# Sums of weight blocks by an adding load, Silu in one activation, and attention masks one unit later

## The chip, the core and the metric

The kernel runs on one core of a Trainium2 chip. The metric is device time of one execution in microseconds (us). Work is spread over engines that each run their own list of instructions in order: TensorE does the matrix products (PE in the profile, with its weight loads shown apart as PEld), VectorE (DVE) does elementwise arithmetic, ScalarE (ACT) does copies, scaling and activation functions, GpSimd (POOL) issues some transfers and makes index patterns, and SyncE (SP) issues most transfers. Semaphores order the engines among each other. An engine that waits for a semaphore does nothing else until it comes.

## The reference

The reference is a two-layer decoder trunk on 256 tokens of width 2048, in float32. Layer 0 mixes tokens by causal pooling over windows of 2, 4, 8 and 16; layer 1 by 16-head attention in three dilated branches. After each mixer stands a residual sum with a layer norm, then a gated feed-forward with a causal convolution of width 3, and a second residual sum and norm:

```python
u = h @ w_up                                   # 2048 -> 2 * 5504
c = conv_b + sum_j shift(u, j) * conv_w[j]     # depthwise, width 3
gate, val = jnp.split(c, 2, axis=-1)
return (jax.nn.silu(gate) * val) @ w_down      # 5504 -> 2048
```

Here silu(x) is x times sigmoid(x). The change touches the loading of `w_down`, the sigmoid of `gate`, and the tables from which attention masks its scores.

## The kernel before

**Units.** All matrix work is cut into units, a list built ahead of time in the order in which they are to run. Most units own one weight block of 512 rows by 512 columns, 1 MB, held as a tile `raw` of 128 partitions by 4 row blocks by 512 columns. To keep float32 accuracy on the TensorE's float32r inputs, each block is split in two: ACT copies `raw` to `wh` (which rounds it) and DVE writes the rest, `raw - wh`, to `wl`. The products then use both parts. In an ordinary unit the copy is line L82 and the subtraction L83; its matmuls are L165 and L166.

**Order.** `run_units` takes one unit after another. At unit i, `ahead(i)` first issues the loads up to unit i+5 (`do_load`, L72, on SP) and then the splits up to unit i+3; then come the unit's matmuls, then whatever was put off with `later(n, ...)` until this unit, then the unit's own follow-up (`post`). Every engine gets its instructions in this written order and runs them in it. There are three `raw` buffers and four pairs `wh`, `wl`, so SP's next load waits until a `raw` has been split, and ACT's next copy waits until TensorE is through with a `wh`.

**Seven products.** For most row blocks of `w_down` the kernel uses a Strassen-like scheme (the Winograd form): a block of activations and a block of weights are each seen as two by two sub-blocks, and seven products of sums of sub-blocks replace eight. The seven products of one weight block are done in two units that share one `raw`: the "a" unit with three of them and the "b" unit with four. The "b" unit has no load of its own. The sums of weight sub-blocks are made in `split_sums`, in place in `raw`. With r11, r12 (first two row blocks, left and right 256 columns) and r21, r22 (last two), the "a" split does: ACT copies r11, r21 and r22 to `wh` (L103, two instructions); DVE subtracts r11 from r12 (L104); DVE makes `wl` (L106, two instructions); DVE subtracts r12 from r22 (L107); DVE subtracts r22 from r11 and r21 at once (L109). The "b" split then copies and subtracts all four (L96 on ACT, L97 on DVE, two each). There are 58 such blocks, 28 in layer 0 and 30 in layer 1.

**Weaving.** The feed-forward's down-projection is done in chunks of row blocks: chunk 0 has blocks 0 to 2, chunk 1 has 3 to 5, chunk 2 has 6 and 7, chunk 3 the rest. Each chunk runs over four column groups, and the units of one column group are woven between four units of the up-projection (`weave`). In chunk 1 the units of one column group run in the order a3 b3 u a4 b4 u a5 b5 u u, where u is an ordinary up-projection unit, and then the next column group begins with a3 again. Below, this run of ten units is called a cycle of chunk 1; there are four in each layer.

**What follows a column group.** After b5, `early_post` combines the seven products' PSUM banks on DVE (L812 to L819) into tiles `w`, `u3` and `u5`, `tm_post` adds other banks to the stream `HT[c]` (L840, L842), and then POOL adds the three tiles onto `HT[c]` by three adding transfers (L271, `accum_op=OP.add`; in the rows of the profile `ht<-w` of 256 KB and twice `ht<-u` of 128 KB). These wait for the DVE instructions just named, and they are written before the loads of the next `ahead`. In the two column groups of layer 1's chunk 3 that have a seven-product block, `early_post` adds on DVE instead (L822 to L826).

**Gate.** After the convolution of a gate block, `three` (L614 to L617) takes the Sigmoid on ACT into a part of tile `u` (L615), and DVE multiplies it by the convolution's result (L616). This is done 22 times. The product with the value half is L672.

**Masks.** Attention adds a table `negm` and multiplies by a table `cnt`. Each is made in three parts, `masks(0)` to `masks(2)`: an IOTA on POOL and ten small DVE instructions (L1147 to L1159). They are put off until the sixth to eighth turn of the attention stage. In the same turn as `masks(0)`, but behind it, stand the last step of the preceding layer norm (`lo(3)`, L286) and the evacuation of the first key group (`norm_evac`, L446 to L449).

Of the kernel before, what the change touches and what calls it, by code (L numbers as in the profile page):

```python
# [12 lines left out]
AF = mybir.ActivationFunctionType  # L13
OP = mybir.AluOpType
# [4 lines left out]
P = 128  # L19
# [13 lines left out]
def trunk(ctx: ExitStack, tc: tile.TileContext, x, pool_w_in, pool_w_grp, pool_scale, pool_w_out,  # L33
          attn_w_q, attn_w_o, shared_w_k, shared_w_v, ffn_w_up, ffn_conv_w, ffn_conv_b, ffn_w_down,
          ln1_g, ln1_b, ln2_g, ln2_b, out):
    nc = tc.nc
    V, A, PE = nc.vector, nc.scalar, nc.tensor
# [14 lines left out]
    units = []  # L52
    state = {"loaded": 0, "split": 0, "done": 0}
    raw, wh, wl = {}, {}, {}
# [4 lines left out]
    def pieces(i, nk):  # L59
        return [slice(k, k + 1) for k in range(nk)] if i < 4 else [slice(0, nk)]  # L60

    def do_load(i, part=None):
        src = units[i][0]
        if src is None:
            return
        nk, n = src.shape[0] // P, src.shape[1]
        if not part:
            raw[i] = rawp.tile([P, nk, n], F32, name=f"raw{i}", tag="raw")
        rows = src.rearrange("(k p) n -> p k n", p=P)
        ks = pieces(i, nk)  # L70
        for s in ks if part is None else ks[1:] if part else ks[:1]:
            nc.sync.dma_start(raw[i][:, s], rows[:, s])  # L72
# [15 lines left out]
    B1, B2, N1, N2 = slice(0, 2), slice(2, 4), slice(0, 256), slice(256, 512)  # L88

    def split_sums(i, kind):  # L90
        h = wh[i] = wp.tile([P, 4, 512], F32R, name=f"wh{i}", tag="wh")
        l = wl[i] = wp.tile([P, 4, 512], F32R, name=f"wl{i}", tag="wl")
        if kind == "b":
            r = raw.pop(i - 1)
            for n in (N2, N1):
                A.copy(h[:, :, n], r[:, :, n])  # L96
                V.tensor_tensor(l[:, :, n], r[:, :, n], h[:, :, n].bitcast(F32), OP.subtract)  # L97
            return
        r = raw[i]
        r11, r12, r22 = r[:, B1, N1], r[:, B1, N2], r[:, B2, N2]  # L100
        parts = [(slice(0, 4), N1), (B2, N2)]
        for k, n in parts:
            A.copy(h[:, k, n], r[:, k, n])  # L103
        V.tensor_tensor(r12, r12, r11, OP.subtract)  # L104
        for k, n in parts:
            V.tensor_tensor(l[:, k, n], r[:, k, n], h[:, k, n].bitcast(F32), OP.subtract)  # L106
        V.tensor_tensor(r22, r22, r12, OP.subtract)  # L107
        both = r[:, :, N1].rearrange("p (b k) n -> p b k n", b=2)
        V.tensor_tensor(both, both, r22.unsqueeze(1).to_broadcast([P, 2, 2, 256]), OP.subtract)  # L109

# [9 lines left out]
    def later(n, fn):  # L120
        if n == 0:
            fn()
        else:
            pending.append([n, fn])

    def run_units(upto):
        while state["done"] < upto:
            i = state["done"]
            ahead(i)
            for fn in before.pop(i, ()):  # L130
                fn()
            mm, post = units[i][1:3]
            mm(wh.pop(i), wl.pop(i))
            ready = [p for p in pending if p[0] <= 1]
            rest = [p for p in pending if p[0] > 1]
            for p in rest:
                p[0] -= 1
            pending[:] = rest
            for p in ready:
                p[1]()  # L140
            if post is not None:
                post()
            state["done"] += 1
# [404 lines left out]
    def ffn(lay):  # L548
# [16 lines left out]
        def evac(ps, nb, mode):  # L565
            fp = pools["ffn"]
            u = pads()

            def tmp():
                return fp.tile([P, T], F32, name="ut", tag="t1", bufs=3)  # L570

            if mode == "x":
                norm_evac(ps, nb, tmp, lambda m: u[:, m, 2:])
                return u
            for m in range(nb):
                t = tmp()
                A.copy(t, ps[m][:, T:])  # L577
                V.tensor_tensor(u[:, m, 2:], ps[m][:, :T], t, OP.add)  # L578
            return u

        def conv(u, blk0, nb, then, quick=False):
            cv = cvec[lay]
            c = pools["ffn"].tile([P, 4, T], F32, name="c", tag="t4")
            for m in range(nb):
                j = blk0 + m
                A.activation(c[:, m, :], u[:, m, 2:], AF.Identity, scale=cv[:, 2, j:j + 1], bias=cv[:, 3, j:j + 1])  # L586

            def tap(i, to):
                for m in range(nb):
                    j = blk0 + m  # L590
                    A.activation(to[:, m, :], u[:, m, i:i + T], AF.Copy, scale=cv[:, i, j:j + 1])  # L591
                V.tensor_tensor(c[:, :nb], c[:, :nb], to[:, :nb], OP.add)

            def second():
                tap(1, pools["ffn"].tile([P, 4, T], F32, name="a", tag="t4"))

            def third():
                tap(0, u[:, :, 0:T])
                then(c)

            for n, fn in ((1, second), (2, third)):
                later(0 if quick else n, fn)
# [6 lines left out]
        def gate_chain(q, nb, mode, ps):  # L609
                u = evac(ps, nb, mode)  # L610

                def gated(c):
                    def three():
                        s = u[:, :nb, 2:]  # L614
                        A.activation(s, c[:, :nb], AF.Sigmoid)  # L615
                        V.tensor_tensor(c[:, :nb], s, c[:, :nb], OP.mult)  # L616
                        gates[q] = c  # L617

                    later(1, three)

                later(1, lambda: conv(u, 4 * q, nb, gated))
# [129 lines left out]
        if lay == 0:  # L751
            rows = [(512 * q, min(512, FF - 512 * q)) for q in (8, 9, 10)]
# [54 lines left out]
    def early_post(c, by_dma):  # L807
        def post(p16, p75):
            w = lnp.tile([P, 512], F32, name="w", tag="fold2")
            u = lnp.tile([P, 256], F32, name="u3", tag="f1")  # L810
            left, right = w[:, :256], w[:, 256:]
            A.copy(left, p16[:, :256])  # L812
            V.tensor_tensor(right, left, p16[:, 256:], OP.add)
            V.tensor_tensor(u, right, p75[:, :256], OP.add)
            y0, y1 = HT[c][:, 0, :], HT[c][:, 1, :]
            if by_dma:
                u5 = lnp.tile([P, 256], F32, name="u5", tag="cs")
                V.tensor_tensor(right, right, p75[:, 256:], OP.add)
                V.tensor_tensor(u5, u, p75[:, 256:], OP.add)  # L819
                ST["onto"] = [(y0, w), (y1[:, :256], u), (y1[:, 256:], u5)]  # L820
                return
            V.tensor_tensor(y0, y0, w, OP.add)  # L822
            y1 = y1.rearrange("p (a n) -> p a n", a=2)
            V.tensor_tensor(y1, y1, u.unsqueeze(1).to_broadcast([P, 2, 256]), OP.add)
            yr = HT[c][:, :, 256:]
            V.tensor_tensor(yr, yr, p75[:, 256:].unsqueeze(1).to_broadcast([P, 2, 256]), OP.add)  # L826
        return post
# [265 lines left out]
    with tc.tile_pool(name="pool", bufs=1) as pp:  # L1093
# [5 lines left out]
        for l in range(2):  # L1099
            n = 80 if l == 0 else 64  # L1100
            r = pp.tile([80, P], F32, name=f"vrow{l}")
# [37 lines left out]
    with tc.tile_pool(name="attn", bufs=1) as ap:  # L1139
        pools["attn"] = ap  # L1140
        for nm in ("cnt", "negm"):
            ST[nm] = ap.tile([P, 3, P], F32, name=nm)

        def masks(i):
            two = ap.tile([P, 2, P], F32, name="dist", tag="t1", bufs=2)
            dist, fm = two[:, 0], two[:, 1]
            nc.gpsimd.iota(dist, pattern=[[-1, P]], base=P * (i == 1), channel_multiplier=1,  # L1147
                           allow_small_or_imprecise_dtypes=True)
            itwo = ap.tile([P, 2, P], I32, name="idist", tag="t1", bufs=2)
            idist, im = itwo[:, 0], itwo[:, 1]  # L1150
            cn = ST["cnt"][:, i, :]
            V.tensor_copy(idist, dist)
            V.tensor_scalar(cn, dist, float(P), None, op0=OP.is_le)
            for dil in (4, 16):
                V.tensor_scalar(im, idist, dil - 1, None, op0=OP.bitwise_and)
                V.tensor_copy(fm, im)
                V.scalar_tensor_tensor(cn, fm, 0.0, cn, op0=OP.is_equal, op1=OP.add)
            V.scalar_tensor_tensor(cn, dist, 0.0, cn, op0=OP.is_ge, op1=OP.mult)
            V.tensor_scalar(ST["negm"][:, i, :], cn, 0.0, NEG, op0=OP.is_equal, op1=OP.mult)  # L1159

        for i in range(3):
            later(6 + i, lambda i=i: masks(i))
        run_units(marks[2])
    with tc.tile_pool(name="ffn1", bufs=4) as fp:
        pools["ffn"] = fp
# [30 lines left out]
```

## Time and profile before

| what | value |
|---|---|
| median of 3 runs | 2048.98 us (2048.14 to 2051.68) |
| profiled execution | 2047.57 us |
| its span, first to last instruction | 2045.8 us |
| PE busy | 2027.3 us (99%) |
| DVE busy | 1699.9 us (83%) |
| ACT busy | 1259.2 us (62%) |
| POOL busy | 75.2 us (4%) |
| granted TensorE clock | 1.0 |

A row of instructions in the profile begins with the line of the code and the engine; then come the operation, the output tile and its inputs, their shapes, the count, and behind a bar the total busy time and the mean duration in ns. A row of waits names who waited for whom, the total in us, how often, and the longest. A row of the timeline begins with its start and duration in us; brackets at its end say how long the engine stood idle before it and what ended that. Times of the timeline are counted from the span's start. "To landing" is the time from the issue of a transfer to its completion.

### The profile page before, as it was taken

Reading aid. Unit: us, or ns where it says so; the run is one execution under the profiler, and the core shown is the slowest. Engines: PE = TensorE matmul, PEld = TensorE weight load, DVE = VectorE, ACT = ScalarE, POOL = GpSimd, SP = SyncE. Lnnn points to the kernel's source line nnn. Section 1 sums busy time; section 2 is a strip of 40 time slices with the busy share of each in tenths; the row PEclk is TensorE's granted clock in tenths of the full one; section 3 lists DMA queues with packets and bytes.
Section 4 is the critical chain, followed back from the end, with each engine's and each line's share of the span. In section 5 each row is a group of like instructions: output and inputs, shape, how many; then the busy total and the mean of one; then the engine's idle time right before and its main releaser. Section 6 shows DMA issues by size and latency. Waiting matters only on the chain. (4 is left out here: it accounts for less than half of the span.)

```text
span 2045.8 us, 31252 instructions
## 1 busy us (share of the span) xinstructions
PE 2027.3 (99%) x12532; PEld 1810.4 (88%) x12532; DVE 1699.9 (83%) x2020; ACT 1259.2 (62%) x1679; POOL 75.2 (4%) x112
## 2 busy tenths in 40 slices
PE   9999999999999999999999999999999999999999
PEld 9899988898888898889888888998888889889987
DVE  6759877888899899889856657787888889999998
ACT  6545686666766676667534434477766676767673
POOL 2000000001000100100000000000010001000100
PEclk9999999999999999999999999999999999999999
DMA  8655466667456757765475555557576646666665
GB/s 267 211 190 185 168 215 191 198 215 223 151 194 216 220 179 223 225 216 172 167 219 182 175 182 172 186 183 210 164 242 200 226 135 205 217 216 193 209 208 184
DMA packets 278305, 405.92 MB, mean 198 GB/s; under 512 B 80414, under 2 KB 95668, under 8 KB 277904
## 3 DMA queue, kind: packets, MB, share of 16 engines
q1 hardware_dynamic: 266144, 389.72, 57.3%
q0 software_dynamic: 11584, 13.55, 4.4%
q8 instruction: 98, 1.61, 0.3%
q10 hardware_dynamic: 432, 0.66, 0.1%
q14 instruction: 47, 0.39, 0.1%
HBM read 380.01 MB, written 2.10 MB: 187 GB/s over the span
## 5 line engine op out<-in xcount | busy, mean ns | idle before, releaser
L165 PE MATMUL acc<-xc,wh 128*128 128x512 f32 x3264 | 1153.4, 396 | 1.7 <-DVE xc L286 1.6
L166 PE MATMUL acc<-xc,wl 128*128 128x256 f32 x3264 | 917.4, 281 | 6.1 <-DVE wl L83 5.4
L83 DVE TENSOR_TENSOR wl<-raw,wh 128x2048 fp32r<-128x2048 f32 (+2 forms) x318 | 686.7, 2167 | 241.3 <-ACT wh L82 240.5
L165 PEld LDWEIGHTS acc<-xc,wh 128*128 128x128 f32 x3264 | 615.7, 189 | 145.4 <-issue 2.7
L82 ACT CAST wh<-raw 128x2048 fp32r<-128x2048 f32 (+2 forms) x318 | 572.9, 1810 | 249.9 <-PE acc L165 124.8
L166 PEld LDWEIGHTS acc<-xc,wl 128*128 128x128 f32 x3264 | 615.4, 189 | 11.5 <-DVE wl L83 11.0
L96 ACT CAST wh<-raw 128x1024 fp32r<-128x1024 f32 x116 | 121.0, 1052 | 88.3 <-DVE raw L107 76.3
L97 DVE TENSOR_TENSOR wl<-raw,wh 128x1024 fp32r<-128x1024 f32 x116 | 137.2, 1219 | 7.7 <-ACT wh L96 7.7
L577 ACT COPY ut<-acc 128x256 f32<-128x256 f32 x164 | 55.0, 370 | 139.9 <-DVE u L578 117.2
L103 ACT CAST wh<-raw 128x1024 fp32r<-128x1024 f32 x116 | 90.8, 831 | 56.0 <-DMA raw<-in_ffn_w_down_dram 36.3
L106 DVE TENSOR_TENSOR wl<-raw,wh 128x1024 fp32r<-128x1024 f32 x116 | 105.6, 952 | 8.2 <-ACT wh L103 8.1
L229 PE MATMUL t<-wh,g 128*128 128x256 f32 x344 | 96.8, 281 | 2.3 <-DVE g L658 2.3
L228 PE MATMUL t<-wl,g 128*128 128x256 f32 x344 | 96.8, 281 | 0.0
L227 PE MATMUL t<-wh,g 128*128 128x256 f32 x344 | 96.7, 281 | 0.0
L586 ACT ACTIVATE c<-u,cv 128x256 f32<-128x256 f32 x172 | 89.5, 593 | 3.7 <-DVE u L578 3.7
L228 PE MATMUL s<-wl,xs 128*128 128x256 f32 x308 | 86.8, 282 | 2.1 <-DVE wl L97 2.1
L227 PE MATMUL s<-wh,xs 128*128 128x256 f32 x308 | 86.1, 280 | 0.0
L229 PE MATMUL s<-wh,xs 128*128 128x256 f32 x308 | 86.0, 279 | 0.0
L271 POOL DMA_DIRECT2D ht<-w x24 | 20.3, 848 | 1733.8 <-DVE ht L838 680.6
L591 ACT ACTIVATE a<-u,cv 128x256 f32<-128x256 f32 x172 | 73.5, 499 | 0.0
L591 ACT ACTIVATE u<-u,cv 128x256 f32<-128x256 f32 x172 | 73.4, 499 | 0.0
L109 DVE TENSOR_TENSOR raw<-raw 128x1024 f32<-128x1024 f32 x58 | 71.1, 1225 | 2.0
(273 smaller groups left out, 3449.0 us busy)
## 6 DMA issues: line engine op xcount, KB each, us to landing
raw<-in_ffn_w_up_dram SPq DMA_DIRECT2D x160, 1024.0 KB, 5.0
raw<-in_ffn_w_down_dram SPq DMA_DIRECT2D x80, 1024.0 KB, 5.7
raw<-in_pool_w_out_dram SPq DMA_DIRECT2D x16, 1024.0 KB, 5.0
raw<-in_shared_w_k_dram SPq DMA_DIRECT2D x16, 1024.0 KB, 5.0
raw<-in_attn_w_q_dram SPq DMA_DIRECT2D x16, 1024.0 KB, 5.2
raw<-in_shared_w_v_dram SPq DMA_DIRECT2D x16, 1024.0 KB, 5.7
raw<-in_attn_w_o_dram SPq DMA_DIRECT2D x16, 1024.0 KB, 5.0
raw<-in_pool_w_in_dram SPq DMA_DIRECT2D x12, 1024.0 KB, 5.5
```

The lines of the kernel that those rows point to most:

```text
L82: A.copy(wh[i][:, s], r[:, s])
L83: V.tensor_tensor(wl[i][:, s], r[:, s], wh[i][:, s].bitcast(F32), OP.subtract)
L96: A.copy(h[:, :, n], r[:, :, n])
L97: V.tensor_tensor(l[:, :, n], r[:, :, n], h[:, :, n].bitcast(F32), OP.subtract)
L103: A.copy(h[:, k, n], r[:, k, n])
L106: V.tensor_tensor(l[:, k, n], r[:, k, n], h[:, k, n].bitcast(F32), OP.subtract)
L165: PE.matmul(ps[m], h[:, k, c], q[:, k, :, :T], start=st, stop=False)
L166: PE.matmul(ps[m][:, :T], l[:, k, c], q[:, k, 0, :T], start=False, stop=sp and not shifted)
L227: PE.matmul(to, xh, h[:, k, n], start=opens and kk == 0, stop=False)
L228: PE.matmul(to, xh, l[:, k, n], start=False, stop=False)
L229: PE.matmul(to, xl, h[:, k, n], start=False, stop=ends and kk == 1)
L591: A.activation(to[:, m, :], u[:, m, i:i + T], AF.Copy, scale=cv[:, i, j:j + 1])
```

## The change

There are three parts.

First, r12 of a seven-product block is no longer made on DVE. The block is loaded by three plain transfers on SP (r12 alone, then r21 with r22, then r11) and one adding transfer on POOL, which reads r11 from memory again and adds it onto r12 where it lies. This transfer has to wait until r12 has landed. r12 now holds the sum instead of the difference, so r22's subtraction is turned round, and signs change in `early_post`: where a tile was added a part of it is now subtracted. In the branch without adding transfers, two instructions of 512 columns become four of 256.

Second, ACT's Sigmoid into a part of `u` and DVE's product with it become one Silu on ACT, in place in `c`.

Third, `masks(0)` to `masks(2)` run one unit later.

```diff
+        if len(units[i]) > 3:
+            r = raw[i]
+            for k, c in ((B1, N2), (B2, slice(0, 512)), (B1, N1)):
+                nc.sync.dma_start(r[:, k, c], rows[:, k, c])
+            nc.gpsimd.dma_start(r[:, B1, N2], rows[:, B1, N1], accum_op=OP.add)
+            return
         ks = pieces(i, nk)
...
-        r11, r12, r22 = r[:, B1, N1], r[:, B1, N2], r[:, B2, N2]
+        r12, r22 = r[:, B1, N2], r[:, B2, N2]
...
-        V.tensor_tensor(r12, r12, r11, OP.subtract)
...
-        V.tensor_tensor(r22, r22, r12, OP.subtract)
+        V.tensor_tensor(r22, r12, r22, OP.subtract)
...
-                        s = u[:, :nb, 2:]
-                        A.activation(s, c[:, :nb], AF.Sigmoid)
-                        V.tensor_tensor(c[:, :nb], s, c[:, :nb], OP.mult)
+                        A.activation(c[:, :nb], c[:, :nb], AF.Silu)
                         gates[q] = c
...
-                V.tensor_tensor(right, right, p75[:, 256:], OP.add)
-                V.tensor_tensor(u5, u, p75[:, 256:], OP.add)
+                V.tensor_tensor(right, p75[:, 256:], right, OP.subtract)
+                V.tensor_tensor(u5, p75[:, 256:], u, OP.subtract)
...
-            V.tensor_tensor(y0, y0, w, OP.add)
-            y1 = y1.rearrange("p (a n) -> p a n", a=2)
-            V.tensor_tensor(y1, y1, u.unsqueeze(1).to_broadcast([P, 2, 256]), OP.add)
+            for y, a, b in ((y0, left, right), (y1, u, u)):
+                V.tensor_tensor(y[:, :256], y[:, :256], a, OP.add)
+                V.tensor_tensor(y[:, 256:], y[:, 256:], b, OP.subtract)
...
-            later(6 + i, lambda i=i: masks(i))
+            later(7 + i, lambda i=i: masks(i))
```

## The prediction

> **What bounds the kernel now.** I read the page's head first, then the waits of TensorE's weight loads, then the waits of ACT.
>
> ```profile
> span 2045.8 us, 31252 instructions
> PE 2027.3 (99%) x12532; PEld 1810.4 (88%) x12532; DVE 1699.9 (83%) x2020; ACT 1259.2 (62%) x1679; POOL 75.2 (4%) x112
> ...
> PEld acc L166 <- DVE wl L83: 11.0, 16, 2.3
> PEld t L229 <- DVE g L658: 3.2, 4, 0.9
> PEld s L228 <- DVE wl L97: 3.0, 5, 1.7
> ...
> ACT wh L103 <- DMA raw<-in_ffn_w_down_dram: 36.3, 16, 4.1
> ```
>
> TensorE is busy for 99% of the span, so a gain can only come from its waits, which are 18.5 us (2045.8 less 2027.3) as the page models the ends of matmuls. The waits of the weight loads say what they are for: the low weight halves (L83, L97) and the low halves of activation sums (L658) come late from DVE, 17.2 us together. DVE is the engine behind TensorE, and the row on L103 adds that ACT, ahead of DVE, stood 36.3 us for blocks of `w_down` that had not landed. So some of these blocks are loaded with no time to spare, and it is these blocks whose loading the change makes longer.
>
> Where do TensorE's waits lie? Asked by stretches, most are in chunk 1 of either layer, whose cycle (a3 b3 u a4 b4 u a5 b5 u u) stands in the kernel's description. First layer 0 from its second cycle on, then the same in layer 1, then one cycle by engine (columns: length, busy PE, PEld, DVE, ACT, POOL, granted clock, share of the DMA engines, GB/s).
>
> ```profile
> PEld acc L166 <- DVE wl L83: 3.4, 5, 1.2
> PEld s L228 <- DVE wl L97: 0.2, 1, 0.2
> ...
> PEld acc L166 <- DVE wl L83: 3.2, 5, 1.2
> PEld s L228 <- DVE wl L97: 0.2, 1, 0.2
> ...
> 589.00:627.40 38.40, 37.90 (x255) 34.44 (x255) 35.96 (x40) 25.72 (x35) 2.58 (x3) 1.00 0.65 206
> ```
>
> That is 7.0 us over three cycles in each layer, 1.2 us a cycle, with DVE busy 35.96 of 38.40 us and the granted clock at full. In this stretch DVE's order of work is the kernel's pace. One cycle in order of time (start, duration), for SP's loads, then DVE, then POOL, and last how long POOL's three adding transfers took:
>
> ```profile
> 576.18 0.37 SPq L72 DMA_DIRECT2D raw<-in_ffn_w_down_dram  x1
> 580.58 0.37 SPq L72 DMA_DIRECT2D raw<-in_ffn_w_down_dram  x1
> 593.29 0.37 SPq L72 DMA_DIRECT2D raw<-in_ffn_w_down_dram  x1
> 614.65 0.37 SPq L72 DMA_DIRECT2D raw<-in_ffn_w_down_dram  x1
> ...
> 573.80 2.35 DVE L97 TENSOR_TENSOR wl<-raw,wh 128x1024 fp32r<-128x1024 f32 x2
> 576.07 4.48 DVE L83 TENSOR_TENSOR wl<-raw,wh 128x2048 fp32r<-128x2048 f32 x2
> 581.33 0.69 DVE L104 TENSOR_TENSOR raw<-raw 128x512 f32<-128x512 f32 x1 [0.77 <-DMA raw<-in_ffn_w_down_dram]
> 582.42 1.83 DVE L106 TENSOR_TENSOR wl<-raw,wh 128x1024 fp32r<-128x1024 f32 x2 [0.40 <-ACT wh L103]
> 584.28 0.69 DVE L107 TENSOR_TENSOR raw<-raw 128x512 f32<-128x512 f32 x1
> 588.38 0.41 DVE L842 TENSOR_TENSOR ht<-ht,t 128x256 f32<-128x256 f32 x1
> 594.52 0.68 DVE L104 TENSOR_TENSOR raw<-raw 128x512 f32<-128x512 f32 x1
> 596.97 0.69 DVE L107 TENSOR_TENSOR raw<-raw 128x512 f32<-128x512 f32 x1
> 609.26 0.69 DVE L107 TENSOR_TENSOR raw<-raw 128x512 f32<-128x512 f32 x1
> ...
> 588.99 0.85 POOL L271 DMA_DIRECT2D ht<-w  x1 [84.92 <-issue]
> 589.52 2.05 POOL L271 DMA_DIRECT2D ht<-u  x2
> ...
> L271 POOL DMA_DIRECT2D ht<-u x2: 1179/1348/1517, 589.5 to 590.1; - x2
> DMA to landing us min/median/max: 3.4/5.0/7.3
> ```
>
> I count from T = 0 at 576.18, when SP issues the a3 block. SP could not do so earlier: L97 of the block before, which held the buffer, ended at 576.15. DVE splits two ordinary blocks until T = 4.4, waits 0.77 us for a3, runs L104, waits 0.40 for ACT, and reaches L107 at T = 8.10. It ends L842 at T = 12.6, whereupon POOL issues the adding transfers at T = 12.8 and is through with them at T = 15.4 (589.52 + 2.05). The second `ht<-u` was issued at 590.1 and landed 7.3 us later, 597.4, T = 21.2; the first landed at 589.5 + 5.0 = 594.5 and `ht<-w` at 592.4, so behind each other they landed 2.1 and 2.9 us apart. DVE reaches L107 of a4 at T = 20.79 and of a5 at T = 33.1. The next a3 is issued at T = 38.47, which is the cycle.
>
> **The change part by part.**
>
> ```profile
> L104 DVE TENSOR_TENSOR raw<-raw 128x512 f32<-128x512 f32 x58 | 39.6, 682 | 5.3 <-DMA raw<-in_ffn_w_down_dram 5.3
> L616 DVE TENSOR_TENSOR c<-u,c 128x1024 f32<-128x1024 f32 (+1 forms) x22 | 26.3, 1194 | 0.2
> ```
>
> *Removed.* L104 goes 58 times at 0.68 us, L616 22 times at 1.19 us: 39.6 + 26.3 = 65.9 us of DVE. Only what stands where DVE paces TensorE counts. Silu for Sigmoid is one activation of the same shape for one on ACT, and I take nothing for it; its cover is that ACT is busy 62% of the span, and if the new function should need more table loads, they would stand there. The signs in `early_post` cost nothing with adding transfers; in the two column groups without them two instructions become four of half the length, late in the last chunk, where no wait of the list above lies, so nothing.
>
> *Added.* Each of the 58 blocks is issued by three instructions on SP instead of one, at 0.37 us each, so its last piece may land up to 0.74 us later; and POOL gets one adding transfer of 256 KB in 256 pieces of 1 KB. Its parts, bounded from rows: the old block of 1 MB, the shortest plain loads, and a POOL issue of nearly as many pieces (86 rows by 3).
>
> ```profile
> raw<-in_ffn_w_down_dram SPq DMA_DIRECT2D x1, 1024.0 KB, 5.1
> ...
> xin<-in_x_dram SPq DMA_DIRECT2D x4, 128.0 KB, 2.8
> ...
> 29.23 1.88 POOL L1108 DMA_DIRECT2D crow<-in_ffn_conv_w_dram  x1
> ```
>
> For a3: r12 is a quarter of the block and first in the queue, so it lands between 2.8 and 5.1 us after its issue; I take 2.9, since nothing is ahead of it. POOL, waiting for it, then needs 1.9 us to issue 256 pieces (row of 258 pieces: 1.88; low end 0.85, the row of `ht<-w`). `ht<-w` landed 3.4 - 0.85 = 2.55 us after POOL was through, with 128 pieces; for the other 128 I add the smaller distance between the transfers above, 2.1. Sum: T = 2.9 + 1.9 + 2.55 + 2.1 = 9.45, where DVE wants it at 8.10: a stall of 1.35 us. Ends: 2.8 + 3.4 = 6.2, no stall; 5.1 + 1.9 + 2.55 + 2.9 = 12.45, a stall of 4.35. L104 of this block saves nothing, since it stood in the wait for the load.
>
> For a4: POOL's order matters. Units are numbered in the order a3 0, b3 1, u 2, a4 3, b4 4, u 5, a5 6, b5 7, u 8, u 9, and the next cycle's a3 10 and a4 13. `ahead(7)` loads up to unit 12, then unit 7's follow-up writes the adding transfers onto the stream, and only `ahead(8)` loads unit 13. SP runs far ahead (it issued a4 at T = 4.4), but POOL cannot: a4's adding load stands behind L271, which waits for L842. POOL comes to it at T = 15.4, and in the queue it lies behind `ht<-u`, which lands at T = 21.2. One more distance of 2.1 us gives T = 23.3; DVE, relieved of L104, wants it at 20.79 - 0.69 = 20.1. The stall is 3.2 us. Ends: landing 3.4 us after POOL is free, T = 18.8, no stall; two distances of 2.9, T = 27.0, a stall of 6.9. A stall of a3 moves DVE and L271 alike, so the two add.
>
> For a5: issued at T = 17.1, used at 33.1. Sixteen microseconds cover all of this, so L104's 0.69 us is a gain. One of two cycles holds an L616: 0.6 us a cycle on average.
>
> The cycle changes by 1.35 + 3.2 - 0.69 - 0.69 - 0.6 = +2.6 us, to 41.0. TensorE needs 38.47 - 1.2 = 37.3, so it does not take over, and all of it is waited for. Behind a stalled L107 stand DVE's later splits, the PSUM evacuations and L842, and behind L107 itself ACT's L96; that is why nothing makes it good within the cycle. Three cycles in each layer: 6 x 2.6 = +15.6 us (ends: -7.0, where TensorE's own need stops the gain, and 6 x 9.3 = +56).
>
> [...]
>
> *Masks.* Ten DVE instructions of `masks(0)` stand ahead of L286, and TensorE waits for L286:
>
> ```profile
> 976.65 0.22 DVE L1152 CAST idist<-dist 128x128 int32<-128x128 f32 x1
> 978.96 1.22 DVE L286 TENSOR_TENSOR xc<-h,xc 128x1024 fp32r<-128x1024 f32 x1
> ...
> 980.30 0.19 PEld L165 LDWEIGHTS acc<-xc,wh 128*128 128x128 f32 x1 [1.89 <-issue]
> ```
>
> L286 follows at 978.96 instead of 976.65, 2.3 us late, and TensorE's wait of 1.89 us ends just after it. One unit later the masks no longer stand there; I take -1.9 (ends -1.9 and 0, if the evacuation behind it is late next). The mask work meets a DVE that is not the pace there, ahead of the first scores.
>
> *The other stretches.*
>
> ```profile
> 573.94 0.19 PEld L229 LDWEIGHTS t<-wh,g 128*128 128x128 f32 x1 [0.90 <-DVE g L658]
> ...
> PEld acc L166 <- DVE wl L83: 3.3, 3, 2.3
> PEld s L228 <- DVE wl L97: 1.7, 1, 1.7
> ```
>
> The first row is the end of chunk 1's first cycle, before any a3 was loaded late: TensorE waits for L658 because DVE is simply behind, and some 2 us less work (three L104) removes that. The list at the head has four such waits of L658, 3.2 us, all at the first seven products of a chunk. Of its 17.2 us there are then left 17.2 - 7.0 - 3.2 - 5.0 = 2.0 us, small waits mostly behind these; I take both, -5.2 (ends: 0 and -5.2). The 5.0 us are those of chunk 2 in layer 0, the next two rows, where a block lands just in time again; what L104 saves there and what stalls like a3's cost I take as equal, so 0 (ends: -5.0 and +6, one microsecond for six such blocks).
>
> **The sum** against the profiled execution of 2047.6 us: 2047.6 + 15.6 - 1.9 - 5.2 = 2056.1. The median of the runs is 1.4 us above that execution, so the forecast is 2057.5, called 2057.
>
> **The rivals.**
>
> *The adding load is hidden* (ends on the other side). It lands as `ht<-w` does, 3.4 us after POOL comes to it, and is not held by what lies in the queue before it. Then both stalls are 0, the cycles give back their 7.0 us, and 2047.6 - 7.0 - 7.1 - 1.4 (two L104 in chunk 2) + 1.4 = 2033.5. For it: 3.4 us repeats for `ht<-w`. Against it: `ht<-u` behind it. It decides from the point where the stalls of a cycle add to less than 3.2 us (2.0 for the cycle, and 7.1/6 for the masks and the other stretches). [...] Chance 0.24.
>
> *Only a4 is late.* r12's detour fits under ACT's and DVE's work for a3, and a4 stalls 3.2 us: the cycle grows by 1.2, six of them by 7.4, and 2047.6 + 7.4 - 7.1 + 1.4 = 2049.3, no change. For it: the a3 stall is the smaller, 1.35 us out of a sum of four estimates. Chance 0.18.
>
> *The queue bounds.* 256 pieces take two distances of 2.9 us, and the plain loads beside them are held up too: stalls of 2 and 6.9 us, a cycle of +6.9, 41 us in six: 2047.6 + 41 - 7.1 + 1.4 = 2083. For it: the share of the DMA engines, 0.65 in the cycle, grows. Chance 0.14.
>
> **How the numbers follow.** The forecast has 0.44. A tenth of its weight and most of the second rival's fall within 0.2% (4 us), which is about what a measurement of this kernel can tell from no change; the first rival is faster. So faster 0.25, same 0.19, slower 0.56. The range leaves out the lower half of the first rival and rather more than half of the third: 2033 to 2080. The forecast's own range is 2051 to 2068.
>
> **What would show it.** Right: L107 waits for the adding load in chunk 1, longer for a4 than for a3; a cycle of 40 to 42 us by SP's a3 issues; POOL's adding load of a4 directly behind L271; TensorE waiting more for L83 and L97 between 589 and 706; L286 no longer behind `masks(0)`. Wrong: L107 without waits, a cycle near 37.5 us, or adding loads that land within 3.4 us of their issue even behind others. The forecast falls if the queue does not serve the transfers in turn, or if DVE is late enough for other reasons to meet the loads.

## The result and the profile after

| what | before | after |
|---|---|---|
| median of 4 runs each | 2048.56 us (2046.43 to 2051.68) | 2099.61 us (2098.3 to 2105.45) |
| ratio | 1 | 1.0254 (95% interval 1.023 to 1.0277) |
| span of the profiled execution | 2045.8 us | 2096.5 us |
| granted TensorE clock, mean | 1.000 | 0.993 |

The change makes the kernel 51 us slower. Slower was forecast, but by 8 us, and 2099.6 lies above the range (2033 to 2080).

In the changed kernel the lines have moved by up to six: L83 is now L89, L97 is L103, L103 and L106 are L109 and L111, L107 is L112, L109 is L114, L271 is L276, L658 is L661. L73 is SP's three plain pieces, L74 POOL's adding load. The head of the page and one of its groups (busy us and mean ns, then the idle time before them and what ended it):

```profile
span 2096.5 us, 31651 instructions
PE 2045.4 (98%) x12532; PEld 1821.0 (87%) x12532; DVE 1643.9 (78%) x1944; ACT 1260.2 (60%) x1679; POOL 146.0 (7%) x170
...
L112 DVE TENSOR_TENSOR raw<-raw 128x512 f32<-128x512 f32 x58 | 40.2, 693 | 60.2 <-DMA raw<-in_ffn_w_down_dram 59.2
```

DVE lost 56.0 us of work (1699.9 to 1643.9) and got 59.2 us of a new wait: L112, the first instruction that needs the sum, waits for the adding load. The waits of the weight loads, of DVE and of ACT say how this reaches TensorE (total us, times, longest):

```profile
PEld acc L171 <- DVE wl L89: 22.9, 13, 2.8
PEld s L233 <- DVE wl L103: 13.2, 15, 2.2
PEld s L232 <- ACT wh L102: 6.6, 7, 2.1
...
DVE raw L112 <- DMA raw<-in_ffn_w_down_dram: 59.2, 29, 3.9
...
ACT wh L109 <- DMA raw<-in_ffn_w_down_dram: 50.6, 21, 5.8
```

The two waits for the low halves, 14.0 us before, are 36.1 us. The wait for ACT in L232 is new: ACT's L102 needs what L112 and L114 make. ACT's own wait for the plain pieces grew from 36.3 to 50.6 us.

Where the time was lost is read from one DVE instruction that both kernels have in every seven-product block, the subtraction from r11 and r21 (L109 before, L114 after). How much later it starts after than before, taken at the ends of the chunks, gives the loss of each. The timeline of DVE before, the last block ahead of chunk 1's second cycle, the last of chunk 1 and the last of chunk 2, in layer 0 and then in layer 1:

```profile
571.39 1.23 DVE L109 TENSOR_TENSOR raw<-raw 128x1024 f32<-128x1024 f32 x1
686.99 1.23 DVE L109 TENSOR_TENSOR raw<-raw 128x1024 f32<-128x1024 f32 x1
839.89 1.23 DVE L109 TENSOR_TENSOR raw<-raw 128x1024 f32<-128x1024 f32 x1
1678.66 1.23 DVE L109 TENSOR_TENSOR raw<-raw 128x1024 f32<-128x1024 f32 x1
1794.40 1.22 DVE L109 TENSOR_TENSOR raw<-raw 128x1024 f32<-128x1024 f32 x1
1942.01 1.23 DVE L109 TENSOR_TENSOR raw<-raw 128x1024 f32<-128x1024 f32 x1
```

The same six blocks after:

```profile
569.75 1.23 DVE L114 TENSOR_TENSOR raw<-raw 128x1024 f32<-128x1024 f32 x1
702.70 1.23 DVE L114 TENSOR_TENSOR raw<-raw 128x1024 f32<-128x1024 f32 x1
859.43 1.22 DVE L114 TENSOR_TENSOR raw<-raw 128x1024 f32<-128x1024 f32 x1
1697.91 1.23 DVE L114 TENSOR_TENSOR raw<-raw 128x1024 f32<-128x1024 f32 x1
1831.87 1.23 DVE L114 TENSOR_TENSOR raw<-raw 128x1024 f32<-128x1024 f32 x1
1992.45 1.23 DVE L114 TENSOR_TENSOR raw<-raw 128x1024 f32<-128x1024 f32 x1
```

The differences are -1.64, 15.71, 19.54, 19.25, 37.47 and 50.44 us. Chunk 1 lost 17.35 in layer 0 and 18.22 in layer 1, together 35.6; chunk 2 lost 3.8 and 13.0, together 16.8; all the rest gained some 2. Now chunk 1's second cycle in layer 0, as the prediction showed it before: SP, DVE, ACT, POOL (start, duration; in brackets the idle time before it and what ended that).

```profile
574.55 1.40 SPq L73 DMA_DIRECT2D raw<-in_ffn_w_down_dram  x3
618.04 1.39 SPq L73 DMA_DIRECT2D raw<-in_ffn_w_down_dram  x3
...
586.30 0.69 DVE L112 TENSOR_TENSOR raw<-raw 128x512 f32<-128x512 f32 x1 [2.60 <-DMA raw<-in_ffn_w_down_dram]
602.04 0.69 DVE L112 TENSOR_TENSOR raw<-raw 128x512 f32<-128x512 f32 x1 [3.14 <-DMA raw<-in_ffn_w_down_dram]
613.72 0.69 DVE L112 TENSOR_TENSOR raw<-raw 128x512 f32<-128x512 f32 x1
...
580.79 1.57 ACT L109 CAST wh<-raw 128x1024 fp32r<-128x1024 f32 x2 [5.11 <-DMA raw<-in_ffn_w_down_dram]
...
577.93 1.19 POOL L74 DMA_DIRECT2D raw<-in_ffn_w_down_dram  x1 [25.46 <-DMA raw<-in_ffn_w_down_dram]
591.63 2.08 POOL L276 DMA_DIRECT2D ht<-u  x2
592.72 2.21 POOL L74 DMA_DIRECT2D raw<-in_ffn_w_down_dram  x1
602.94 1.20 POOL L74 DMA_DIRECT2D raw<-in_ffn_w_down_dram  x1 [8.02 <-DMA raw<-in_ffn_w_down_dram]
```

From T = 0 at 574.55, POOL comes to a3's adding load at T = 3.4 and DVE gets it at T = 11.75, 2.60 us after it was ready for it. a4's adding load stands directly behind L276's `ht<-u`, and DVE waits 3.14 us for it. a5's is not waited for. The cycle is 43.49 us long (618.04 - 574.55) where it was 38.47. How long the transfers took, in short windows around their issues: a3's plain pieces; a3's adding load, and beside it the next block of `w_up` and a piece of a4; a4's adding load; a5's.

```profile
raw<-in_ffn_w_down_dram SPq DMA_DIRECT2D x2, 256.0 KB, 4.0
raw<-in_ffn_w_down_dram SPq DMA_DIRECT2D x1, 512.0 KB, 5.0
...
raw<-in_ffn_w_up_dram SPq DMA_DIRECT2D x1, 1024.0 KB, 8.4
raw<-in_ffn_w_down_dram POOLq DMA_DIRECT2D x1, 256.0 KB, 8.3
raw<-in_ffn_w_down_dram SPq DMA_DIRECT2D x1, 256.0 KB, 7.5
...
raw<-in_ffn_w_down_dram POOLq DMA_DIRECT2D x1, 256.0 KB, 9.2
...
raw<-in_ffn_w_down_dram POOLq DMA_DIRECT2D x1, 256.0 KB, 4.1
```

The same 256 KB take 4.1 us for a5, issued at 602.94 while SP issues no load until 606.36, 8.3 for a3 beside a block and the pieces of another, and 9.2 for a4 behind `ht<-u` and beside the next plain loads. The loads beside a3's are slower as well: the same block of `w_up`, issued 2.2 us after a3 in both kernels, took 8.4 us after and 6.1 before.

```profile
raw<-in_ffn_w_up_dram SPq DMA_DIRECT2D x1, 1024.0 KB, 6.1
```

### The profile page after: what moved, and what is told of

It is laid out like the page before. It is cut to its first block, busy times and chain, and to the rows that moved or that the text cites. A ratio compares the mean times of both kernels' runs of the same rounds, so it can differ in the third digit from the quotient of the medians.

```text
span 2096.5 us, 31651 instructions
## 1 busy us (share of the span) xinstructions
PE 2045.4 (98%) x12532; PEld 1821.0 (87%) x12532; DVE 1643.9 (78%) x1944; ACT 1260.2 (60%) x1679; POOL 146.0 (7%) x170
## 5 line engine op out<-in xcount | busy, mean ns | idle before, releaser
L171 PE MATMUL acc<-xc,wl 128*128 128x256 f32 x3264 | 922.3, 283 | 18.8 <-DVE wl L89 18.7
L89 DVE TENSOR_TENSOR wl<-raw,wh 128x2048 fp32r<-128x2048 f32 (+2 forms) x318 | 687.1, 2168 | 257.0 <-ACT wh L88 253.0
L171 PEld LDWEIGHTS acc<-xc,wl 128*128 128x128 f32 x3264 | 620.6, 190 | 23.4 <-DVE wl L89 22.9
L102 ACT CAST wh<-raw 128x1024 fp32r<-128x1024 f32 x116 | 121.0, 1052 | 126.1 <-DVE raw L112 94.9
L74 POOL DMA_DIRECT2D raw<-in_ffn_w_down_dram x58 | 75.5, 1302 | 1436.0 <-DMA raw<-in_ffn_w_down_dram 1047.5
L103 DVE TENSOR_TENSOR wl<-raw,wh 128x1024 fp32r<-128x1024 f32 x116 | 137.4, 1220 | 7.7 <-ACT wh L102 7.7
L111 DVE TENSOR_TENSOR wl<-raw,wh 128x1024 fp32r<-128x1024 f32 x116 | 105.8, 954 | 43.0 <-ACT wh L109 42.8
L109 ACT CAST wh<-raw 128x1024 fp32r<-128x1024 f32 x116 | 90.8, 832 | 75.6 <-DMA raw<-in_ffn_w_down_dram 50.6
L232 PE MATMUL t<-wh,g 128*128 128x256 f32 x344 | 97.2, 283 | 0.7 <-DVE u L822 0.7
L232 PE MATMUL s<-wh,xs 128*128 128x256 f32 x308 | 87.2, 283 | 5.2 <-ACT wh L102 5.2
L112 DVE TENSOR_TENSOR raw<-raw 128x512 f32<-128x512 f32 x58 | 40.2, 693 | 60.2 <-DMA raw<-in_ffn_w_down_dram 59.2
```

Source lines behind the costliest of these rows:

```text
L89: V.tensor_tensor(wl[i][:, s], r[:, s], wh[i][:, s].bitcast(F32), OP.subtract)
L171: PE.matmul(ps[m][:, :T], l[:, k, c], q[:, k, 0, :T], start=False, stop=sp and not shifted)
L232: PE.matmul(to, xh, h[:, k, n], start=opens and kk == 0, stop=False)
```

## The experiments

The theory after the result: the load part costs everything; a4 is late by its place behind L276, a3 by the detour over a second transfer among other loads, and in chunk 2 it is as with a3. The rivals: another part of the change costs too; the adding itself is what is slow; the three pieces are; every adding load costs, wherever it is.

### The parts by themselves

Four kernels hold one part or two each. From the kernel before, with Silu alone, with the masks alone, and with both:

```diff
-                        s = u[:, :nb, 2:]
-                        A.activation(s, c[:, :nb], AF.Sigmoid)
-                        V.tensor_tensor(c[:, :nb], s, c[:, :nb], OP.mult)
+                        A.activation(c[:, :nb], c[:, :nb], AF.Silu)
...
-            later(6 + i, lambda i=i: masks(i))
+            later(7 + i, lambda i=i: masks(i))
```

The fourth is the changed kernel with these two parts undone, so the load alone.

> The kernel before with Silu and the later masks, and the blocks loaded and summed as before. Theory (all of the loss comes from the adding load): the wait of 1.9 us behind the masks goes, and Silu takes 0.6 us of DVE work from a cycle of chunk 1, six times, so 2042 to 2046 us where the kernel before takes 2048.6. Rival (Silu or the masks cost something of their own): over 2050.

> Only the changed loading and summing, with Sigmoid and the masks as before. Theory: the kernel after plus what Silu and the masks save, 2101 to 2108 us. Rival (Silu or the masks cost something): below 2098.

> Masks one unit later alone, all else as before. The prediction gave 1.9 us: 2045 to 2048.5 us. Rival (the wait moves to another operation): 2048 to 2050 us.

> Silu in place of Sigmoid and the product alone, all else as before. With masks and Silu together at 2042.7 and the masks' 1.9: 2043 to 2046.5 us. Rival (the time of the two together was the masks'): 2047 to 2049 us.

| kernel | median us | ratio to before (95%) |
|---|---|---|
| Silu and masks | 2042.72 | 0.997 (0.9959 to 0.9981) |
| load alone | 2103.06 | 1.0262 (1.0248 to 1.0276) |
| masks alone | 2049.16 | 1.0002 (0.9993 to 1.0011) |
| Silu alone | 2040.62 | 0.9959 (0.9945 to 0.9972) |

The load part alone is 54 us slower; against the kernel with Silu and masks it costs 2099.6 - 2042.7 = 56.9 us. Silu alone gains 8 us, more than was forecast for it, below its range. Its activation takes the time of the Sigmoid's, 1061 ns against 1063 in ACT's group before (L615), with two table loads of 1283 ns at this line in both. The group of ACT with Silu alone:

```profile
L614 ACT ACTIVATE c<-c 128x1024 f32<-128x1024 f32 x20 | 21.2, 1061 | 2.9 <-DVE c L592 2.3
```

The masks alone do nothing: the rival held. The trace shows why. The wait of 1.89 us at 980.30 is gone, and another one came. The timeline of the weight loads with the masks alone, and the same place before:

```profile
1038.63 0.19 PEld L165 LDWEIGHTS acc<-xc,wh 128*128 128x128 f32 x1 [1.51 <-DVE o L1045]
```

```profile
1035.88 0.19 PEld L165 LDWEIGHTS acc<-xc,wh 128*128 128x128 f32 x1 [0.20 <-DVE o L1045]
```

L1045 evacuates the first attention output, which needs scores and so the masks. TensorE waits for it 1.31 us longer, which is most of the 1.89. The steps between the masks and L1045 were not followed one by one.

### One block of a cycle at a time

In these kernels `units` carries the number of the row block, and only the blocks in `ADDED` are loaded in pieces with the adding load; the others are loaded as before and summed on DVE (with the new sign). Silu and masks are as in the changed kernel, so the kernel with Silu and masks, 2042.7, is what they are compared with.

```diff
+ADDED = (3,)
...
-        if len(units[i]) > 3:
+        if len(units[i]) > 4 and units[i][4] in ADDED:
...
+        if units[i][4] not in ADDED:
+            V.tensor_tensor(r12, r12, r11, OP.add)
```

`ADDED` is (3,), (4,), (5,), (6, 7) and (1, 2, 5). Blocks 3, 4, 5 are a3, a4, a5.

> The adding load for a3 alone. Theory: the six steps of a3 in the trace after add to 18.2 us; with some loss of granted clock 2055 to 2068 us. Rival (a3's wait comes only from what the other adding loads put into the queue): under 2050.

> The adding load for a4 alone. Theory: the six steps of a4 in the trace after add to 21.0 us, and it is behind a4 that TensorE's gaps stand close together and the clock fell; 2060 to 2075 us. Rival: under 2052.

> The adding load for a5 alone (block 5 of chunk 1, which has time to spare), one plain load and DVE's own addition for all other blocks; Silu and the later masks stay. The kernel with Silu and masks alone took 2042.7 us. Theory: a5's adding load is hidden and takes 0.6 us from each of eight cycles, of which TensorE's waits in six cycles let something through, so 2038 to 2042 us. Rival (any adding load costs, by its traffic beside the plain loads): over 2046.

> The adding load for blocks 6 and 7 (chunk 2) alone. Theory: 3.8 us in layer 0 and 12.7 us in layer 1 were lost there in the trace after, so 2054 to 2062 us. Rival (that loss came from chunk 1, whose stalls left no lead): under 2048.

> The adding load for blocks 1, 2 and 5 alone, DVE's own addition for the others; Silu and the masks as in the changed kernel. Theory (the load costs where its landing falls later than DVE is ready for it, and block 5's does not): chunk 0, where blocks 1 and 2 lie, was not taken apart so far; its steps in the changed kernel's trace are small, so 2034 to 2042 us, like the kernel with block 5 alone (2037.2). Rival (each adding load costs by the second round of its bytes, wherever it is): two more blocks in two layers at some 23 us a pair, half of that if chunk 0 is less full: 2050 to 2080 us.

| adding load for | median us | ratio to before (95%) | against 2042.7 |
|---|---|---|---|
| a3 | 2066.0 | 1.0087 (1.0074 to 1.0101) | +23.3 |
| a4 | 2066.43 | 1.0087 (1.0073 to 1.01) | +23.7 |
| a5 | 2037.21 | 0.9944 (0.993 to 0.9957) | -5.5 |
| chunk 2 (blocks 6 and 7) | 2060.77 | 1.0059 (1.0046 to 1.0072) | +18.0 |
| blocks 1, 2 and 5 | 2035.48 | 0.9935 (0.9922 to 0.9947) | -7.2 |

The first four add up to 59.5 us, where the whole load part costs 56.9: the parts stand nearly alone. The same instruction and the same 256 KB cost 23 us at a3, in six of whose eight blocks DVE waits, and gain 5.5 at a5. So the rival by which every adding load costs falls; a5's 2037.2 us lies even just under the range given for it. With blocks 1 and 2 in chunk 0 added, the kernel stays as fast: the intervals overlap, so no gain is shown there, and the 5.0 us that DVE waits in four of chunk 0's sixteen blocks are no loss either. One wait of each, on DVE's timeline: with a3 alone, then with a4 alone.

```profile
587.18 0.69 DVE L115 TENSOR_TENSOR raw<-raw 128x512 f32<-128x512 f32 x1 [2.32 <-DMA raw<-in_ffn_w_down_dram]
```

```profile
599.65 0.69 DVE L115 TENSOR_TENSOR raw<-raw 128x512 f32<-128x512 f32 x1 [3.58 <-DMA raw<-in_ffn_w_down_dram]
```

The six waits with a4 alone lie between 3.58 and 4.21 us; those with a3 alone between 1.88 and 4.67.

### Why a4 is late

In the first kernel, L276's three transfers go one unit later in chunks 0 and 1, so that a4's adding load stands ahead of them in POOL's order. The rest is the changed kernel.

```diff
-                for y, z in ST.pop("onto", ()):
-                    nc.gpsimd.dma_start(y, z, accum_op=OP.add)
+                onto = ST.pop("onto", ())
+
+                def put():
+                    for y, z in onto:
+                        nc.gpsimd.dma_start(y, z, accum_op=OP.add)
+
+                later(1 if onto and len(r0s) == 3 and len(seven) == 3 else 0, put)
```

> The kernel after, but in chunks 0 and 1 the three adding transfers onto the stream are written one unit later, so that POOL comes to a4's adding load before them. Theory (a4 is late because its load stands behind these transfers in POOL's order and in the queue): a4's wait of 3.1 to 3.9 us goes in all six cycles, 18 to 23 us, so 2074 to 2083 us; a3's wait stays at 2 to 4 us. Rival (the load is slow wherever it stands, because the transfers beside it fill the DMA engines): a4 still waits 2 us or more and the time stays above 2090.

2081.52 us, 1.0161 of before (1.0147 to 1.0175): 18 us of the 51 are gone. Counted against before, DVE's sum of a4 is now as late as that of a3 ahead of it (a step of -0.06 us in five cycles and 0.22 in the sixth, where the changed kernel has 3.5 on average), and the total of the waits on the adding load falls from 59.2 to 40.5 us. The steps of a3 stay at 2.3 to 4.6 us. This left open whether a4 profits only from the delay that a3 causes ahead of it. The second kernel has no a3: `ADDED` is (1, 2, 4, 5), L276 later as above, the masks in their old place. Beside it ran the same without a4 and with L276 in its old place, `ADDED` (1, 2, 5).

> The adding load for blocks 1, 2 and 5, and Silu; the masks where they were before. Theory (the masks one unit later only move TensorE's wait: the 1.9 us behind L286 go, 1.3 us come behind the attention output, and work around it shifts; beside Silu the move cost 2.1 us): 2032 to 2034.5 us, some 2 us under the 2035.5 with the masks moved. Rival (the 2.1 us came from something else between the two kernels): 2035 to 2037.5 us.

> As the kernel with blocks 1, 2, 5 and Silu, with the adding load for the fourth block too, and the three transfers of L271 one unit later in chunks 0 and 1, so that the fourth block's adding load stands ahead of them in POOL's order. Theory (the fourth block is late through its place behind L271 alone): its wait goes and DVE gains another 0.69 us a cycle, at most 4 us in six cycles: 2029 to 2035 us. Rival (the detour and the second round of bytes cost the fourth block too): 1 to 2 us in each of six cycles, 2040 to 2047 us.

The kernel before took 2050.61 us beside these two, so the expectations in microseconds, made from 2048.6, stand some 2 us too low. Without a4: 2037.78 us, ratio 0.994 (0.9927 to 0.9952); with a4 and L276 later: 2037.23 us, ratio 0.9941 (0.9928 to 0.9955). The rival, 1 to 2 us in each of six cycles, falls: a4's adding load costs nothing once it stands ahead of L276 (L282 here), as on POOL's timeline:

```profile
585.01 1.19 POOL L75 DMA_DIRECT2D raw<-in_ffn_w_down_dram  x1 [32.26 <-DVE w L824]
587.46 0.89 POOL L282 DMA_DIRECT2D ht<-w  x1 [1.26 <-issue]
```

No block of chunk 1 waits for an adding load there. Ahead of L282 the load also runs mostly before the next plain loads, which SP issues from 589.52 on: a4's landed after 4.0 to 5.0 us there in the six cycles, against 9.7 to 10.4 with a4 alone in the old place. So that POOL's order decides is shown; how much of the wait was the queue behind `ht<-u` and how much the plain loads beside it was not separated. But a4's adding load gains nothing either, where the theory had up to 4 us: at a4 DVE's next step waits 0.45 us for ACT in each of the six cycles, so that most of the 0.69 us that DVE saves is spent there, and the step of a block is only -0.06 us.

```profile
593.48 1.83 DVE L114 TENSOR_TENSOR wl<-raw,wh 128x1024 fp32r<-128x1024 f32 x2 [0.45 <-ACT wh L110]
```

For the masks, the kernel with blocks 1, 2, 5 has 0.994 with the masks in their old place and 0.9935 with them later. The interval of each holds the other's value; the rival held here too, and moving the masks can't be told from no change anywhere.

### What makes a3 late

Two kernels take a3's detour apart. In the first, the three plain pieces stay and DVE makes the sum as before; there is no adding load.

```diff
-            nc.gpsimd.dma_start(r[:, B1, N2], rows[:, B1, N1], accum_op=OP.add)
...
-        r12, r22 = r[:, B1, N2], r[:, B2, N2]
+        r11, r12, r22 = r[:, B1, N1], r[:, B1, N2], r[:, B2, N2]
...
+        V.tensor_tensor(r12, r12, r11, OP.add)
```

> The kernel after with its three plain loads for a block, but without the adding load: DVE adds r11 onto r12, as it subtracted it before. Theory: the three pieces cost little, under 1 us in each cycle of chunk 1, so 2043 to 2051 us. Rival (it is the cutting of the load in three that is late): 2060 or more.

In the second, POOL's transfer stays in its place and size but does not add, so the sum is missing from the output.

```diff
-            nc.gpsimd.dma_start(r[:, B1, N2], rows[:, B1, N1], accum_op=OP.add)
+            nc.gpsimd.dma_start(r[:, B1, N2], rows[:, B1, N2])
```

> The fourth transfer of every block stays where it is, on POOL, behind the three plain ones, with the same 256 KB; it overwrites its tile instead of adding to it, and reads the piece that goes to that tile (so the sum is left out of the output: block 12 keeps its own values). Theory (the step comes from a second round of the same bytes behind the plain pieces and beside the other loads, not from the adding): the time stays within 2090 to 2105 us, and the wait of DVE on this transfer in chunk 1 stays 3 to 4 us for the third and fourth block. Rival (the adding itself is slow, a read and a write of the tile for each element): the transfer lands in about half of the 8.3 us, the waits fall under 1.5 us, and the time falls to 2050 to 2075 us.

The pieces alone: 2051.82 us, 1.0011 of before (1.0003 to 1.002), so 9.1 us over the kernel with Silu and masks and just above the range given (its eleven runs spread from 2047.0 to 2054.1). The plain second load: 2077.17 us, 1.0134 (1.012 to 1.0148), between the theory's 2090 to 2105 and the rival's 2050 to 2075. So both were half right, and the waits show which half. DVE's timeline with the plain second load, a3 and a4 of two cycles:

```profile
585.44 0.69 DVE L112 TENSOR_TENSOR raw<-raw 128x512 f32<-128x512 f32 x1 [1.52 <-DMA raw<-in_ffn_w_down_dram]
601.40 0.69 DVE L112 TENSOR_TENSOR raw<-raw 128x512 f32<-128x512 f32 x1 [3.36 <-DMA raw<-in_ffn_w_down_dram]
...
670.74 0.69 DVE L112 TENSOR_TENSOR raw<-raw 128x512 f32<-128x512 f32 x1 [0.50 <-DMA raw<-in_ffn_w_down_dram]
686.39 0.69 DVE L112 TENSOR_TENSOR raw<-raw 128x512 f32<-128x512 f32 x1 [3.06 <-DMA raw<-in_ffn_w_down_dram]
```

a4 waits as long without the adding, 3.36 and 3.06 us, so the adding is not what makes it late. a3's waits fall from 2.60 and 2.52 to 1.52 and 0.50. By the steps of DVE's sum, over those of the kernel with Silu and masks and as means of the six a3: the three pieces 1.2 us, the plain second load 2.0, the adding load 3.4. So of a3's step 1.2 us are the pieces, 0.8 the second round and 1.4 the adding, if they stack. That the adding costs something by itself shows at a5, with no load issued beside it: in the six cycles the plain second load lands 3.0 to 3.1 us after its issue, the adding one 4.0 to 4.2. The plain transfer is also issued faster (0.72 us against 1.19) and was cut into fewer packets: POOL's queue has (16224 - 11584)/58 = 80 more a block, and 272 with the adding load. Before, that queue had 11584 packets and 4.4%. The page's row of it (packets, MB, share of the DMA engines) with the plain second load, and then in the changed kernel:

```profile
q0 software_dynamic: 16224, 28.76, 6.6%
```

```profile
q0 software_dynamic: 27360, 28.76, 9.0%
```

Why the adding transfer is the slower one was not taken apart; no run here varied the number or the size of the packets alone. Beside SP's loads POOL's transfer takes twice as long (8.3 us at a3, 4.1 at a5), and a load beside it is slower too (8.4 us for the block of `w_up`, 6.1 before).

## Why the prediction was wrong

The sign and chunk 1's mechanism were right, the size was not: 8.5 us forecast, 51 measured. By the timeline the error lies in chunk 1 (15.6 forecast, 35.6 measured), chunk 2 (0 and 16.8) and the rest (-7.1 forecast; the spans differ by 50.7 us, which leaves 50.7 - 35.6 - 16.8 = -1.7). Chunk 1's 35.6 lies within the ends that the prediction gave for it (-7.0 and +56), chunk 2's 16.8 outside its own (-5.0 and +6). It took both: with only chunk 2 mended the forecast would have been 2074 us, with only chunk 1 mended 2077, both within the range.

*a3, mis-sized.* The prediction had a stall of 1.35 us, between 0 and 4.35; the steps of the six are 1.7 to 3.7 us, 3.0 on average. Of its four terms r12's landing was nearly right (2.9 us, POOL came at 3.4), POOL's issue too high (1.9; 1.2 measured), and the way from there to the landing far too low: 2.55 + 2.1 = 4.65 against 11.75 - 3.4 - 1.2 = 7.1 us. It was taken from `ht<-w`, beside which a plain load runs only in the last 1.3 us (591.09 to 592.43), and widened by the distance of two `ht<-u`. a5's adding load, with no load issued beside it, took 4.1 - 1.2 = 2.9 us for the same way, so what the term lacked is the traffic beside a3 and not the adding alone. The later plain pieces were named (0.74 us) and then left out of the sum: DVE itself is ready for the sum at T = 9.15, not 8.10.

*a4, right in its place and its wait, wrong in its gain.* The wait was forecast at 3.2 us; the six are 3.14 to 3.89. The landing was forecast at T = 23.3; it is 27.4, and less the 3.65 us that a3 had moved everything, 23.8. But the step of a block is +3.05 to +3.87 us instead of 3.2 - 0.69: L104's time isn't gained at a4, since DVE then waits for ACT (0.45 to 0.52 us before L111, where before it did not wait).

*a5, right.* Sixteen microseconds cover its load; each step is -0.6 us.

*Chunk 2, the step that failed.* "What L104 saves there and what stalls like a3's cost I take as equal, so 0", with six stalls of one microsecond as the upper end. The changed kernel has eleven waits of L112 there, 19.2 us together, up to 3.86 each, and the chunk costs 16.8 us by the timeline and 18.0 by itself. That is nearly three times the upper end. The prediction had quoted that this chunk's blocks land just in time, and its own price for a3 was above the microsecond that it put there. The longest of these waits belongs to an adding load that runs beside two blocks of `w_up` (issues from 763.5 to 767):

```profile
raw<-in_ffn_w_up_dram SPq DMA_DIRECT2D x2, 1024.0 KB, 9.1
raw<-in_ffn_w_down_dram POOLq DMA_DIRECT2D x1, 256.0 KB, 9.5
```

So this one is a3's case, with more beside it. Why layer 1 loses 13.0 us there and layer 0 only 3.8, with waits of 11.6 and 7.6 us, is open.

*Masks, right in the trace and wrong in time.* The wait behind L286 went, its 1.9 us did not: the bound of 0 was in the text, with the evacuation behind L286 as what would be late next. It was the attention output, some 56 us further on.

*Silu, too small.* 8.0 us measured alone. In chunk 1's cycles it moves DVE by 1.0 and 1.2 us over three of them, less than the 0.6 a cycle; in chunk 2, where the sum has nothing for it, by 3.1 and 1.5 us. The rest was not followed.

*The other stretches.* The waits of L658 went as forecast, 3.2 to 0.4 us. Of the 5.4 us that are missing outside the two chunks, 1.9 are the masks, and 1.7 are a wait for the first weights at 9.48 us, which the profiled execution of before doesn't have and that of the masks alone has too; some 1.8 us are open.

*The granted clock, not in the sum.* See below; it is a part of the times above and not one beside them.

Of the rivals, "the queue bounds" comes nearest: its cycle was to grow by 6.9 us, and it grew by 5.9. It had the plain loads beside the adding load held up, as they are, but put its time on a4, where it lies on both. With its 41 us and chunk 2's 16.8 the forecast would have been 2100. "The adding load is hidden" needed landings of 3.4 us after the issue; the median of the 58 is 5.9.

## What to carry to other kernels

Price an added transfer by a transfer that runs beside the same traffic, not by one of the same kind elsewhere: here the same 256 KB took 4.1 us for a5 and 7.4 to 10.0 us for a3 and a4 among other loads, and a block of `w_up` beside one took 8.4 us instead of 6.1. Of a step that repeats in several stages, ask in each stage how much time lies between issue and use, and keep it only where there is enough: for a5 the adding load gains, in chunk 0 it costs nothing, and blocks 1, 2 and 5 with Silu and the masks moved take 2035.5 us (0.9935 of before), faster than both kernels; for a4 it costs nothing if it is issued ahead of L276's transfers (2037.2 us with it, 2037.8 without). And a wait that a reordering removes has only gone when the end moved: look for the next one that has the same length.

## What the runs showed of the hardware

TensorE's granted clock fell to half in the changed kernel, though the longest wait of a weight load there is 2.8 us (L171). In the cycle after the one shown, the weight load that follows the longest gap:

```profile
654.81 0.29 PEld L171 LDWEIGHTS acc<-xc,wl 128*128 128x128 f32 x1 [2.14 <-DVE wl L89]
```

After a gap of 2.14 us, with three shorter ones (0.95, 1.09 and 0.57 us) in the seven microseconds before it, the clock is at half for 3.41 us, from 654.34 to 657.75 (last row of the windows below). Thirteen windows of 4 us are below 0.97; 4 us times what each lacks to 1 gives 14 us in all. Before, the clock falls only at the very end of the span, by 0.4 us so counted. Nearly the same gaps a cycle earlier, 0.43, 1.09, 0.65 and 2.14 us around 610, left the clock at full.

The trace tells the two apart. Ahead of its end it holds eight such times of 3.41 us at half, and their starts lie whole multiples of 3.413 us apart (13, 63, 318, 331, 344, 374 and 393 after the first). Cut at these multiples, the gaps around 610 fall into two windows, and most of those ahead of 654.34 into one (length, busy PE and count, granted clock, share of the DMA engines, GB/s):

```profile
606.55:609.97 3.42, 2.03 (x15) 1.00 0.73 251
609.97:613.38 3.41, 2.52 (x14) 1.00 0.56 171
650.93:654.34 3.41, 1.69 (x12) 1.00 0.83 287
654.34:657.75 3.41, 2.94 (x9) 0.50 0.59 183
```

In this trace half clock follows each of the nine windows in which TensorE is idle for 1.72 us or more, and none with 1.53 or less (the ends of matmuls, and so the idle times, are modelled). The trace of before, cut in the same way from its one start of half clock at 2044.91, has a window with 1.81 us idle (846.83 to 850.24, PE busy 1.60) and the clock still at full behind it, so no one figure parts the windows of both traces, and what makes the clock fall was not shown. How much of the loss these 14 us are is open. Of the 50.7 us by which the span grew, TensorE's busy time for the same 12532 matmuls takes 18.1 (2027.3 to 2045.4) and its idle time 32.6, but no run separates what of the 18.1 is the clock. With a3 alone the mean granted clock of the profiled run is 1.0 (it falls only at the very end of the span, by 1.0 us), and the cost is 23.3 us all the same, so the clock is not what makes that load dear.
